# Scores of a windowed attention: the products with the keys' low halves on 64 rows of the array, two heads in different PSUM banks

## The chip, the cores and the metric

The kernel runs on one core of one Trainium2 chip. The metric is the device time of one execution in microseconds (us). Before the change the median of 3 runs is 1161.12 us (1160.22 to 1161.37). The engines are named as in the profile: PE is TensorE (the matrix array; PEld are its weight loads), DVE is VectorE, ACT is ScalarE, POOL is GpSimd, SP issues DMAs. L701 is line 701 of the kernel before.

## The reference

A decoder trunk of two layers over 512 tokens with 1024 features, all in fp32. Layer 0 mixes tokens by a gated position mix in chunks of 128, then a gated MLP with a short convolution, then a gated embedding. After it keys and values are made once. Layer 1 attends to them in a sliding window of 128 tokens, with 16 query heads in 4 groups that share 4 key heads of 64 features. The part that bears on the change is the attention:

```python
def mixer_b(xn, w_q, sinks, w_o, kblk, vblk):
    q = (xn @ w_q).reshape(B, nb, BLOCK, N_KV_HEADS, GQA_GROUP, HEAD_DIM)
    scores = jnp.einsum('bnikgd,bnjkd->bnkgij', q, kblk) * (HEAD_DIM ** -0.5)
    ...
    scores = scores - slopes[:, :, None, None] * dist
    scores = jnp.where(valid[None, :, None, None], scores, -jnp.inf)
    m = jnp.maximum(jnp.max(scores, axis=-1, keepdims=True), sink)
    e = jnp.exp(scores - m)
    probs = e / (jnp.sum(e, axis=-1, keepdims=True) + jnp.exp(sink - m))
    out = jnp.einsum('bnkgij,bnjkd->bnikgd', probs, vblk)
    return out.reshape(B, S, N_Q_HEADS * HEAD_DIM) @ w_o
```

## The kernel before

Every fp32 operand of a large product is split in two float32r tiles, a high half and the rest, the low half, and a product is the sum of three: high by high, low by high, high by low. `mm3` (L176 to L184) and `mm3t` (L186 to L195) do this for the dense layers; weights are streamed from HBM into raw tiles (L135), and split by ACT (L155) and DVE (L156) a few units ahead of their use.

The attention is done in 16 steps, 4 groups of heads by 4 blocks of 128 queries. `scores(i)` makes the scores of the 4 heads of one group for one block, `weights(i)` divides by the sums, `turn(i)` transposes the weights on TensorE (L733) and splits them, and `mix(i)` multiplies by the values (L756). They are staggered: in round i of the loop come `scores(i)`, then a piece of other work from `fill(i)` (projections of later queries, `values`, and in the last rounds parts of the output product), then `mix(i - 2)`, `turn(i - 1)` and `weights(i)`. Scores, turns and weights are given a high priority, so the program's scheduler may put them ahead of the filler; the order on an engine is fixed when the program is built, and each engine works in that order.

In `scores` a head's contraction is only 64 features long, so the 128 rows of the array hold two things for it. The tile `q` of head e (of 4 in its group) has the high half of its 64 features on one side of the partitions, `sides[e % 2]` (0 to 63 or 64 to 127), and their low half on the other side (L593 to L608). The keys' high half `kh` and low half `kl` are kept twice, on both sides (L579 to L584). So one product of 128 rows, `q` by `kh` (L698), gives high by high plus low by high, and a second, `q` by `kl` (L699), gives high by low plus low by low. A block of scores has 256 keys (the block before and the own one), or 128 for the first block. One PSUM bank holds the scores of two heads, 0 and 1 in the first, 2 and 3 in the second, 256 columns each. A bank is taken from a pool of 8 that all parts of the kernel share.

After a head's two products one DVE instruction (L701) adds the distance penalty, masks, and reduces to the head's smallest negated score, `neg`; in the program it stands between this head's products and those of the next. Then ACT takes the exponential of each head with its sum (L706), and `ds` gathers what the sink adds (L709, L710).

The order of heads that the scheduler made of this in most steps: products of heads 0 and 2 first, then, once the reduction of head 0 has read its bank, head 1, and then head 3.

Of the kernel before, what the change touches and what calls it, by code (L numbers as in the profile page):

```python
# [13 lines left out]
P = 128  # L14
# [12 lines left out]
GQ = HEADS // GROUPS  # L27
# [21 lines left out]
def tile_yoco(ctx: ExitStack, tc: tile.TileContext, t, out: bass.AP, out_b: bass.AP):  # L49
    nc = tc.nc  # L50
# [10 lines left out]
    def psum(name):  # L61
        return mmp.tile([P, S], F32, tag="mm", name=name)
# [250 lines left out]
    def slope(hd):  # L313
        return 2.0 ** (-8.0 * (hd + 1) / HEADS)
# [152 lines left out]
    far = const.tile([P, 2 * P], F32, name="far")  # L467
# [40 lines left out]
    for c in range(4):  # L508
# [4 lines left out]
        for j in range(2):  # L513
# [7 lines left out]
            for b in range(NC):  # L521
                nc.tensor.matmul(sp[:, b * P : (b + 1) * P], zv[b][:, m * P : (m + 1) * P], wsT[:, m, :],
                                 start=True, stop=True)
# [33 lines left out]
    kh = [mp.tile([P, 2, S], F32R, tag=f"m{j}", name=f"kh{j}") for j in range(2)]  # L557
    kl = [mp.tile([P, 2, S], F32R, tag=f"m{2 + j}", name=f"kl{j}") for j in range(2)]
    sides = [slice(0, HD), slice(HD, P)]
# [50 lines left out]
    qs = {0: []}  # L610
# [73 lines left out]
    def scores(i):  # L684


        g, n = steps[i]
        k0 = 0 if n else P
        nk = 2 * P - k0
        t0 = (n - 1) * P + k0  # L690
        pr = mp.tile([P, GQ, 2 * P], F32, tag=f"m{4 + i % 2}", name=f"pr{i}")
        neg = at.tile([P, GQ], F32, tag="neg", bufs=2, name=f"neg{i}")
        for e in range(GQ):
            if e % 2 == 0:
                sc = psum(f"sc{i}_{e}")
            o = sc[:, (e % 2) * 256 : (e % 2) * 256 + nk]
            q = qs[g][e][:, n * P : (n + 1) * P]
            nc.tensor.matmul(o, q, kh[g // 2][:, g % 2, t0 : t0 + nk], start=True, stop=False)  # L698
            nc.tensor.matmul(o, q, kl[g // 2][:, g % 2, t0 : t0 + nk], start=False, stop=True)  # L699
            hd = GQ * g + e  # L700
            nc.vector.tensor_tensor_reduce(out=pr[:, e, :nk], in0=far[:, k0:], in1=o, scale=-slope(hd),  # L701
                                           scalar=nsink[:, hd : hd + 1], op0=ALU.add, op1=ALU.min,
                                           accum_out=neg[:, e : e + 1])
        sm = at.tile([P, GQ], F32, tag="sm", bufs=2, name=f"sm{i}")
        for e in range(GQ):
            nc.scalar.activation(pr[:, e, :nk], pr[:, e, :nk], AF.Exp, bias=neg[:, e : e + 1], scale=-1.0,  # L706
                                 accum_out=sm[:, e : e + 1])
        ds = at.tile([P, GQ], F32, tag="ds", bufs=2, name=f"ds{i}")
        nc.vector.tensor_add(ds, sink[:, GQ * g : GQ * (g + 1)], neg)  # L709
        nc.scalar.activation(ds, ds, AF.Exp)  # L710
        live[i] = (pr, nk, sm, ds)
# [57 lines left out]
    for i in range(last + 2):  # L769
        if i < last:  # L770
            with tc.high_priority():
                scores(i)
        fill(i)
        if i >= 2:
            mix(i - 2)
        if 0 <= i - 1 < last:
            with tc.high_priority():
                turn(i - 1)
        if i < last:
            with tc.high_priority():  # L780
                weights(i)
# [199 lines left out]
```

## Time and profile before

| | |
|---|---|
| median of 3 runs | 1161.12 us |
| the profiled execution | 1160.82 us |
| its span, from the first to the last instruction | 1159.1 us |
| mean granted TensorE clock | 0.998 |
| high products, L698: 48 of 256 columns, 16 of 128 | 589.2 to 688.8 us |
| reductions, L701 | 591.2 to 689.4 us |

The times on the last two lines count from the start of the span, as all times of the trace do. A row of a timeline has the start, the duration, the engine, the line, the operation, output and inputs by the program's names, and the shape: 128*128 128x256 is a stationary operand of 128 by 128 and a moving one of 256 columns. Records of products overlap each other, since the array is pipelined and their ends are modelled; how far apart two starts lie is what a product costs. Where an engine was idle before an instruction, the brackets at the end of the row name the time and what released it.

### The profile page before, as it was taken

Reading aid. Unit: us, or ns where it says so; the run is one execution under the profiler, and the core shown is the slowest. Engines: PE = TensorE matmul, PEld = TensorE weight load, DVE = VectorE, ACT = ScalarE, POOL = GpSimd, SP = SyncE. Lnnn points to the kernel's source line nnn. Section 1 sums busy time; section 2 is a strip of 40 time slices with the busy share of each in tenths; the row PEclk is TensorE's granted clock in tenths of the full one; section 3 lists DMA queues with packets and bytes.
Section 4 is the critical chain, followed back from the end, with each engine's and each line's share of the span. In section 5 each row is a group of like instructions: output and inputs, shape, how many; then the busy total and the mean of one; then the engine's idle time right before and its main releaser. Section 6 shows DMA issues by size and latency. Waiting matters only on the chain.

```text
span 1159.1 us, 13846 instructions
## 1 busy us (share of the span) xinstructions
PE 1145.6 (99%) x5464; PEld 962.0 (83%) x5464; DVE 742.9 (64%) x1165; ACT 530.7 (46%) x860; POOL 78.4 (7%) x87
## 2 busy tenths in 40 slices
PE   9999999999999999999999999999999999999997
PEld 7888888888888888888888888888888888888896
DVE  7356477763676367556877876677636773675665
ACT  6534344431344244544667874544413432344542
POOL 2000300000000000031200002100000000000222
PEclk9999999999999999999999999999999999999999
DMA  9321322322322323232133214232232232224302
GB/s 321 122 75 73 109 77 106 109 76 107 109 67 97 109 92 120 82 109 107 37 92 110 77 53 174 80 109 85 97 109 84 90 100 109 91 89 148 109 1 73
DMA packets 30736, 115.42 MB, mean 100 GB/s; under 512 B 3016, under 2 KB 14928, under 8 KB 21200
## 3 DMA queue, kind: packets, MB, share of 16 engines
q1 hardware_dynamic: 29552, 113.37, 28.9%
q10 hardware_dynamic: 1120, 1.18, 0.3%
q8 instruction: 43, 0.70, 0.2%
q14 instruction: 21, 0.17, 0.0%
HBM read 108.24 MB, written 2.11 MB: 95 GB/s over the span
## 4 chain that ended last, share of the span: by engine, by line
PE 95%; DVE 2%; DMA 1%; ACT 1%; issue 1%; POOL 0%; SPq 0%; POOLq 0%; ACTq 0%
PE up L184 14%; PE up L182 14%; PE up L183 14%; PE d L183 8%; PE d L184 8%; PE d L182 8%; PE gate L182 2%; PE gate L183 2%; PE gate L184 2%; PE pv L756 1%; PE o L182 1%; PE v L193 1%; PE v L194 1%; PE o L183 1%; PE o L184 1%; PE u L182 1%
## 5 line engine op out<-in xcount | busy, mean ns | idle before, releaser
L156 DVE TENSOR_TENSOR wl<-wraw,wh 128x1024 fp32r<-128x1024 f32 (+2 forms) x197 | 239.3, 1217 | 135.0 <-ACT wh L155 134.5
L155 ACT CAST wh<-wraw 128x1024 fp32r<-128x1024 f32 (+1 forms) x196 | 202.3, 1034 | 265.9 <-PE d L183 131.5
L182 PE MATMUL up<-nf00h,wh 128*128 128x512 f32 x352 | 137.2, 390 | 0.0
L182 PE MATMUL up<-nf10h,wh 128*128 128x512 f32 x352 | 137.1, 389 | 0.0
L184 PE MATMUL up<-nf00h,wl 128*128 128x512 f32 x352 | 137.0, 389 | 0.0
L184 PE MATMUL up<-nf10h,wl 128*128 128x512 f32 x352 | 137.0, 389 | 0.0
L183 PE MATMUL up<-nf00l,wh 128*128 128x512 f32 x352 | 136.9, 389 | 0.0
L183 PE MATMUL up<-nf10l,wh 128*128 128x512 f32 x352 | 136.9, 389 | 0.0
L182 PE MATMUL d<-ah,wh 128*128 128x512 f32 x352 | 136.9, 389 | 0.0
L183 PE MATMUL d<-al,wh 128*128 128x512 f32 x352 | 136.9, 389 | 0.0
L184 PE MATMUL d<-ah,wl 128*128 128x512 f32 x352 | 136.9, 389 | 0.0
L351 ACT ACTIVATE c<-hs,vec 128x512 f32<-128x512 f32 x88 | 71.6, 816 | 71.7 <-DVE hs L347 71.1
L352 DVE SCALAR_TENSOR_TENSOR c<-hs,vec,c 128x511 f32<-128x511 f32 x88 | 65.8, 749 | 34.6 <-ACT c L351 34.5
L327 DVE TENSOR_TENSOR h<-h,d 128x512 f32<-128x512 f32 x56 | 38.5, 687 | 73.7 <-PE d L184 73.7
L240 ACT CAST ah<-a 128x512 fp32r<-128x512 f32 x44 | 27.4, 623 | 109.5 <-DVE a L357 109.4
L182 PEld LDWEIGHTS up<-nf10h,wh 128*128 128x128 f32 x352 | 66.1, 188 | 13.8
L183 PEld LDWEIGHTS up<-nf00l,wh 128*128 128x128 f32 x352 | 66.1, 188 | 13.8
L182 PEld LDWEIGHTS d<-ah,wh 128*128 128x128 f32 x352 | 66.1, 188 | 13.8
L183 PEld LDWEIGHTS up<-nf10l,wh 128*128 128x128 f32 x352 | 66.1, 188 | 13.7
L183 PEld LDWEIGHTS d<-al,wh 128*128 128x128 f32 x352 | 66.1, 188 | 13.7
L184 PEld LDWEIGHTS up<-nf00h,wl 128*128 128x128 f32 x352 | 66.1, 188 | 13.7
L184 PEld LDWEIGHTS d<-ah,wl 128*128 128x128 f32 x352 | 66.1, 188 | 13.7
(337 smaller groups left out, 2089.4 us busy)
## 6 DMA issues: line engine op xcount, KB each, us to landing
wraw<-in_w_up SPq DMA_DIRECT2D x44, 1024.0 KB, 4.8
wraw<-in_w_down SPq DMA_DIRECT2D x16, 896.0 KB, 4.6
wraw<-in_w_down SPq DMA_DIRECT2D x8, 1024.0 KB, 4.9
wraw<-in_w_u SPq DMA_DIRECT2D x4, 1024.0 KB, 5.7
wraw<-in_w_out SPq DMA_DIRECT2D x4, 1024.0 KB, 4.8
wraw<-in_w_gate SPq DMA_DIRECT2D x4, 1024.0 KB, 4.8
wraw<-in_w_q SPq DMA_DIRECT2D x4, 1024.0 KB, 5.6
wraw<-in_w_o SPq DMA_DIRECT2D x4, 1024.0 KB, 5.4
```

The source lines that it names most:

```text
L155: nc.scalar.copy(wh[:, :n], src)
L156: nc.vector.tensor_sub(wl[:, :n], src, wh[:, :n].bitcast(F32))
L182: nc.tensor.matmul(ps, wh[:, a:b], xh, start=st, stop=False)
L183: nc.tensor.matmul(ps, wh[:, a:b], xl, start=False, stop=False)
L184: nc.tensor.matmul(ps, wl[:, a:b], xh, start=False, stop=en)
L193: nc.tensor.matmul(ps, xh[:, s], wh[:, a:b], start=st, stop=False)
L194: nc.tensor.matmul(ps, xl[:, s], wh[:, a:b], start=False, stop=False)
L240: nc.scalar.copy(hi, src)
L327: nc.vector.tensor_add(h[m], h[m], ps)
L351: nc.scalar.activation(c, hs, AF.Identity, bias=v("conv_b", l * 2 * NJ + col), scale=cw[2])
L352: nc.vector.scalar_tensor_tensor(c[:, 1:], hs[:, : S - 1], cw[1], c[:, 1:], op0=ALU.mult, op1=ALU.add)
L756: nc.tensor.matmul(ps, lhs, rhs[:, :, e, :], start=first, stop=end)
```

## The change

In `scores` both banks are taken at the start, and the heads are dealt to them in turn: 0 and 2 in the first, 1 and 3 in the second. All eight products come first, in the order of the list: with `kh` for heads 0 and 1, with `kl` for heads 0 and 1, and the same for heads 2 and 3. Those with `kh` use all 128 rows as before. Those with `kl` use only the 64 partitions of `sides[e % 2]`, where the head's high half lies: head 0 on partitions 0 to 63 and head 1 on 64 to 127, one after the other into different banks. The product of the query's low half with the keys' low half is so left out. The four reductions follow after the eight products.

```diff
+        banks = [psum(f"sc{i}_{b}") for b in range(2)]
+        out_ = [banks[e % 2][:, e // 2 * 256 : e // 2 * 256 + nk] for e in range(GQ)]
+        cols = slice(n * P, (n + 1) * P)
+        for e in (0, 1, 4, 5, 2, 3, 6, 7):
+            me = slice(0, P) if e < GQ else sides[e % 2]
+            ks = (kh if e < GQ else kl)[g // 2]
+            nc.tensor.matmul(out_[e % GQ], qs[g][e % GQ][me, cols], ks[me, g % 2, t0 : t0 + nk],
+                             start=e < GQ, stop=e >= GQ)
         for e in range(GQ):
-            if e % 2 == 0:
-                sc = psum(f"sc{i}_{e}")
-            o = sc[:, (e % 2) * 256 : (e % 2) * 256 + nk]
-            q = qs[g][e][:, n * P : (n + 1) * P]
-            nc.tensor.matmul(o, q, kh[g // 2][:, g % 2, t0 : t0 + nk], start=True, stop=False)
-            nc.tensor.matmul(o, q, kl[g // 2][:, g % 2, t0 : t0 + nk], start=False, stop=True)
             hd = GQ * g + e
-            nc.vector.tensor_tensor_reduce(out=pr[:, e, :nk], in0=far[:, k0:], in1=o, scale=-slope(hd),
+            nc.vector.tensor_tensor_reduce(out=pr[:, e, :nk], in0=far[:, k0:], in1=out_[e], scale=-slope(hd),
                                            scalar=nsink[:, hd : hd + 1], op0=ALU.add, op1=ALU.min,
                                            accum_out=neg[:, e : e + 1])
```

## The prediction

> **What bounds the kernel now.** I read the page first: the table of engines, and the shares of the chain that ended last.
>
> ```profile
> PE 1145.6 (99%) x5464; PEld 962.0 (83%) x5464; DVE 742.9 (64%) x1165; ACT 530.7 (46%) x860; POOL 78.4 (7%) x87
> ...
> PE 95%; DVE 2%; DMA 1%; ACT 1%; issue 1%; POOL 0%; SPq 0%; POOLq 0%; ACTq 0%
> ```
>
> TensorE (PE) has work nearly always, and 95% of the chain is its own. So the change is worth what it takes from, or adds to, TensorE's time in the one stage that it touches; time of other engines counts only where TensorE waits for it. Next, the table of stretches, for the attention stage and for its busiest quarter. Columns: length, then busy time and count of PE, PEld (weight loads), DVE, ACT, POOL, then granted clock, DMA share and GB/s.
>
> ```profile
> 664.00:690.00 26.00, 24.86 (x161) 21.78 (x160) 22.06 (x83) 21.34 (x72) 0.00 (x0) 1.00 0.21 62
> ...
> 589.00:702.00 113.00, 109.66 (x701) 97.21 (x700) 88.80 (x296) 85.73 (x258) 0.00 (x0) 1.00 0.28 82
> ```
>
> Here TensorE lacks 113.00 - 109.66 = 3.34 us by its records, and those overlap each other, so the real slack is larger. DVE reaches 22.06/26.00 = 85% and ACT 21.34/26.00 = 82% from 664 to 690: these two are close behind TensorE, closer than their 64% and 46% over the whole span say. The clock is full, so it plays no part. The third view is the line of the products with the keys' high halves, with what TensorE waited for ahead of them.
>
> ```profile
> L698 PEld LDWEIGHTS sc<-kh,q x64: 186/188/193, 589.2 to 688.8; 128*128 128x128 f32 x64
> L698 PE MATMUL sc<-kh,q x64: 220/306/388, 589.3 to 689.0; 128*128 128x256 f32 x48, 128*128 128x128 f32 x16
> ...
>   DVE neg L701: 4.2, 11
>   issue: 2.1, 2
>   DVE q L598: 1.8, 2
>   DMA q<-qf: 1.6, 2
> ```
>
> There are 64 such products: 48 with 256 columns (12 steps of 4 heads) and 16 with 128 (the first step of each of the 4 groups). The largest wait, 4.2 us in 11 places, is for "DVE neg L701": the reduction of another head. It comes from the layout: two heads share a PSUM bank, and the second head's product is held until the reduction has read the first out of that bank.
>
> **The change, part by part.** *(1) The low products themselves.* 64 products stay 64. Their columns stay, only rows 64 to 127 or 0 to 63 are dropped, so each alone takes the time it took. A gain needs two of them to run at once. This is the pace of products with 256 columns, a waiting one among them:
>
> ```profile
> 613.04 0.28 PE L193 MATMUL vv<-wh,n10h 128*128 128x256 f32 x1
> 613.16 0.28 PE L194 MATMUL vv<-wh,n10l 128*128 128x256 f32 x1
> 613.28 0.28 PE L195 MATMUL vv<-wl,n10h 128*128 128x256 f32 x1
> 613.49 0.38 PE L698 MATMUL sc<-kh,q 128*128 128x256 f32 x1
> 613.72 0.28 PE L699 MATMUL sc<-kl,q 128*128 128x256 f32 x1
> 613.83 0.28 PE L193 MATMUL vv<-wh,n10h 128*128 128x256 f32 x1
> ```
>
> Unhindered they start 0.12 us apart (613.04, 613.16, 613.28). And this is the pace of weight loads where products with 128 columns leave them no cover:
>
> ```profile
> 590.46 0.19 PEld L698 LDWEIGHTS sc<-kh,q 128*128 128x128 f32 x1 [0.98 <-DVE q L598]
> 590.57 0.19 PEld L699 LDWEIGHTS sc<-kl,q 128*128 128x128 f32 x1
> 590.68 0.19 PEld L194 LDWEIGHTS vv<-wh,n10l 128*128 128x128 f32 x1
> 590.79 0.19 PEld L195 LDWEIGHTS vv<-wl,n10h 128*128 128x128 f32 x1
> ```
>
> One load follows another after 0.11 us, and every low product still needs its own load. If two half-height loads also go one after the other, a pair costs 2 x 0.11 = 0.22 us against 2 x 0.12 = 0.24: it saves 0.02 us, over the 24 pairs of 256 columns about 0.5 us, and nothing over the 8 pairs of 128 columns, which loads bound already. If two half-height loads and both products go at once, each pair saves a whole slot: 24 x 0.12 + 8 x 0.11 = 3.8 us. Those are the ends for this term. No row shows two loads at once, and the nearest rows show them in file, so I take 0.5 us. The Trainium skill ("TensorEngine Tiling (Array Packing)", Key Properties) says that different tiles of the array can run loads and matmuls in parallel; by it this term would be the 3.8 us, which is the second rival. No row here has a half-height product, so the trace can't say.
>
> Neighbours in the program needn't be neighbours on the engine. The order on TensorE at 611.56:
>
> ```profile
> 611.56 0.36 PE L698 MATMUL sc<-kh,q 128*128 128x256 f32 x1
> 611.76 0.28 PE L699 MATMUL sc<-kl,q 128*128 128x256 f32 x1
> 611.88 0.28 PE L698 MATMUL sc<-kh,q 128*128 128x256 f32 x1
> 612.00 0.27 PE L733 MATMUL tr<-ident,pr 128*128 128x128 f32 x1
> 612.03 0.36 PE L699 MATMUL sc<-kl,q 128*128 128x256 f32 x1
> 612.23 0.38 PE L733 MATMUL tr<-ident,pr 128*128 128x128 f32 x2
> ```
>
> A transpose of the step before has slipped between the high and the low product of one head. Where one slips between two low products, that pair has no partner; so even with parallel loads some of the 3.8 us goes.
>
> *(2) Going to half height and back.* With the new order a step goes from full rows to half rows and back twice: 4 x 16 = 64 switches. The nearest switch in this trace is to a part of the columns, the two transposes "turned" with 8 stationary columns (128*8):
>
> ```profile
> 146.25 0.39 PE L184 MATMUL d<-ush,wl 128*128 128x512 f32 x1
> 146.48 0.38 PE L543 MATMUL turned<-ident,vec 128*8 128x128 f32 x2
> 146.62 0.48 PE L182 MATMUL up<-nf00h,wh 128*128 128x512 f32 x1
> 146.93 0.40 PE L183 MATMUL up<-nf00l,wh 128*128 128x512 f32 x1
> ...
> 691.59 0.87 PE tr L733 x8
> ```
>
> The last row, from the chain, prices a transpose at 0.87/8 = 0.11 us, and the first two rows price a product with 512 columns at 0.23. From 146.25 to 146.93 are two such products and two such transposes: 2 x 0.23 + 2 x 0.11 = 0.68 us, and 0.68 us passed. Leaving and re-entering the full array cost nothing there, nor did "turned" wait for the record before it to end at 146.64. So I take 0. The upper bound: had a switch to let the array run empty, it would cost what a 256-column record is longer than its slot, 0.28 - 0.12 = 0.16 us, and with a load that can't start early 0.10 more (next part); 64 x 0.26 = 16.6 us. The Trainium skill (same page, Key Properties) states that changing the tiling mode drains the array; by that rule the sum would be higher by the 10 us worked out in the third rival. The rows at 146.48 don't bear it out for columns; for rows nothing here shows it.
>
> *(3) The waits inside a step.* All eight products of a step now come ahead of its four reductions, so no product waits for a reduction of its own step. That takes away the 4.2 us. It takes away something else: at 613.49 the product that waited runs 613.72 - 613.49 = 0.23 us to the next instead of 0.12. Its load couldn't start ahead of the wait, so 0.11 us of load is exposed. At most two products a step wait like that, 32 x 0.11 = 3.5 us. So the term lies between 0 (every wait comes back elsewhere) and 4.2 + 3.5 = 7.7 us; below nothing it could go only by the new waits of part (4). I take the middle, 3.8 us: what TensorE does right after these products are transposes and value products whose inputs DVE and ACT make, and those two, at 85% and 82% of the stage's end now, would stand near 90% if the stage shrank by 5 us, so some of the waits return under other names.
>
> *(4) What is added.* Head 0's reduction used to need two products; now, as banks are guarded whole (that is why the second head waits today), it needs all four of its bank, the last of which is the seventh issued: five more slots, 0.6 us later. Queued behind it on DVE are the step's other reductions, and ACT's exponentials wait for them. In return the reductions run without a stop: in the chain, one from 667.93 releases a subtraction, then a DMA, then TensorE:
>
> ```profile
> 667.93 0.48 DVE pr L701
> 668.42 0.60 DVE qf L603
> 669.05 2.83 DMA q<-qf
> 672.02 0.30 PE sc L698
> ...
> L701 DVE CUSTOM_DVE_ANT_0 pr<-far,sc,nsink x64: 337/475/483, 591.2 to 689.4; 128x256 f32<-128x256 f32 x48, 128x128 f32<-128x128 f32 x16
> ```
>
> Four reductions at 0.48 us are 1.9 us in file; today the second pair starts only after another round of products. I set 0.6 us later at the start against an earlier end, at 0 for TensorE; what covers it is the filler of projections and merges between the steps. Without that cover it would be 16 x 0.6 = 9.6 us lost, but the filler stays as it is. The first step of a group also has its queries by DMA (1.6 us of waits above): heads 2 and 3 there need later queries than heads 0 and 1, before as after, so that stays. Both banks are taken at once rather than one by one: the second is wanted one product sooner, 0.12 us, against banks that were held over two rounds; 0. No DMA, no instruction of DVE, ACT, POOL or SP is added or removed, so no queue is passed.
>
> *The sum.* The profiled execution took 1160.82 us, of which 1159.1 is its span. 1160.82 - 0.5 - 3.8 = 1156.5 us. The median of the runs is 0.3 us above that execution, so 1156.8; I forecast 1157.0 us, 4.1 us or 0.36% below the median.
>
> **The rivals.** *The waits come back* (0.2): the 4.2 us reappear ahead of transposes and value products, for DVE and ACT. For it speaks their 85% and 82%; against it, the idle time ahead of transposes in the groups of the stage (the last number), which is nothing today:
>
> ```profile
> L733 PE MATMUL tr<-ident,pr 128*128 128x128 f32 x102 | 17.0, 273 | 0.0
> ```
>
> Time: 1161.1 - 0.5 = 1160.6, and anything down to 2.3 us below the median.
>
> *The pairs do run side by side* (0.18): then 3.8 us in place of 0.5, and with the waits 1161.1 - 3.8 - 3.8 = 1153.5 us. Against it speak the loads in file at 590.46 and the transpose inside a pair at 612.00.
>
> *Half height costs* (0.2), the slower side: each switch between full and half rows lets the array run empty or exposes a load. It decides from the point where a switch costs more than (3.8 + 0.5)/64 = 0.07 us. With an exposed load alone, 64 x 0.11 = 7.0 us: 1161.1 + 7.0 - 3.8 = 1164.3. With the drained tail of 0.16 instead, 10.2 us: 1167.5 (the skill's rule of the drain gives this one). Against it: "turned" paid nothing. For it: that was columns, and a load for half the rows may have to leave the other half alone until its product has started.
>
> *The change doesn't do what it says*, that is, no two low products ever overlap, is inside my forecast: that counts on 0.5 us of it only.
>
> **How the numbers follow.** The forecast has 0.42, the waits that come back 0.2, side by side 0.18, half height costs 0.2. The forecast's own range, by the ends of part (3) less what returns, is 1154.5 to 1159.0. The range for 8 in 10 runs from 1153.0, which takes in the side-by-side case, to 1165.0, which takes in the cheaper half of the slower rival; left out are its drained half and some of the far end below, together under 0.2. About 0.2% (2.3 us) is what a measurement of this kernel can tell from no change. Faster by more than that: the forecast's 0.42 less 0.03 at its upper end, plus 0.18, so 0.57. Within it: most of the waits that come back plus that 0.03, 0.22. Slower: 0.21.
>
> **What would show it.** In the changed profile the high products' list of waits has no "DVE neg" of the own step, and the time before them falls from 4.2 us to under 1; if transposes or value products show new waits on DVE or ACT of some 3 us, the first rival holds. Two low products of one pair that start within 0.02 us, with the next product 0.12 us after, mean side by side; starts 0.11 apart mean loads in file. A high product that starts 0.2 us or more after a low one with no wait named means that half height costs. The last value product of the stage starts here:
>
> ```profile
> 701.50 0.28 PE L756 MATMUL pv<-pts,vtl 128*128 128x256 f32 x1
> ```
>
> From the first score product at 589.3 that is 112.2 us; the forecast is wrong if this stretch isn't shorter by 2 us at least.

## The result, and the profile after

The changed kernel takes 1170.02 us (median of 5 runs, 1169.16 to 1171.11), the kernel before 1161.37 us in the same runs: 1.0075 times as long, 95% interval 1.0064 to 1.0086, so 8.7 us slower. The forecast was 1157.0 us. The profiled execution took 1171.11 us, its span 1169.4 us. Its table of engines:

```profile
PE 1157.5 (99%) x5464; PEld 965.3 (83%) x5464; DVE 742.5 (63%) x1165; ACT 529.1 (45%) x860; POOL 78.2 (7%) x87
```

The counts are those of before and the other engines' times are within 2 us of them on DVE and ACT; TensorE (PE) is busy 12 us longer with the same 5464 products. The line of the score products, now L701, shows what replaced the waits:

```profile
L701 PEld LDWEIGHTS sc<-kh,q x64: 186/190/329, 589.4 to 696.9; 128*128 128x128 f32 x64
L701 PE MATMUL sc<-kh,q x64: 220/314/387, 589.6 to 696.9; 128*128 128x256 f32 x48, 128*128 128x128 f32 x16
L701 PEld LDWEIGHTS sc<-kl,q x64: 182/183/183, 589.8 to 697.2; 64*128 64x128 f32 x64
L701 PE MATMUL sc<-kl,q x64: 322/380/385, 589.8 to 697.2; 64*128 64x256 f32 x48, 64*128 64x128 f32 x16
...
  DVE q L598: 2.2, 4
  issue: 1.2, 4
  DMA q<-qf: 0.2, 1
```

"DVE neg" is gone from the list: the 4.2 us of waits for reductions went, as meant (what that number adds up is told further down). But the low products (64*128) have a median record of 380 ns, where those on all rows had 282, though half of the array's rows have nothing to do. The order of products in the third step, on TensorE and on its weight loads, shows why:

```profile
614.59 0.48 PE L701 MATMUL sc<-kh,q 128*128 128x256 f32 x2
615.00 0.38 PE L701 MATMUL sc<-kl,q 64*128 64x256 f32 x2
615.31 0.50 PE L701 MATMUL sc<-kh,q 128*128 128x256 f32 x2
615.74 0.38 PE L701 MATMUL sc<-kl,q 64*128 64x256 f32 x1
616.05 0.33 PE L737 MATMUL tr<-ident,pr 128*128 128x128 f32 x1
616.31 0.38 PE L701 MATMUL sc<-kl,q 64*128 64x256 f32 x1
616.62 0.44 PE L737 MATMUL tr<-ident,pr 128*128 128x128 f32 x2
616.82 0.36 PE L760 MATMUL pv<-pts,vth 128*128 128x256 f32 x1
```

```profile
615.00 0.19 PEld L701 LDWEIGHTS sc<-kl,q 64*128 64x128 f32 x2
615.31 0.30 PEld L701 LDWEIGHTS sc<-kh,q 128*128 128x128 f32 x2
615.74 0.18 PEld L701 LDWEIGHTS sc<-kl,q 64*128 64x128 f32 x1
```

Two things can be read here. The two low products at 615.00 fill one record's time, 0.38 us for both, and their two loads take 0.19 us for both, the time of one: they do run side by side. And the loads behind a change of rows begin with their product (615.00 and 615.00, 615.31 and 615.31) instead of ahead of it; from the pair at 615.00 to the next product are 0.31 us, where a slot, the time from one start to the next, is 0.12. This is the sign that the prediction named for its third rival: a high product that starts 0.2 us or more after a low one, with no wait named. In the second half of the step a transpose at 616.05 has come between the two low products, so this pair is two products alone, and the step has six changes of rows where the order in the kernel's text has four. The stage, from the first score product to the last value product, runs here from 589.56 to this row:

```profile
711.89 0.28 PE L760 MATMUL pv<-pts,vtl 128*128 128x256 f32 x1
```

That is 122.3 us against 112.2 before, 10.1 us longer; the two profiled spans differ by 1169.4 - 1159.1 = 10.3 us, so the loss lies in this stage.

### The profile page after: what moved, and what is told of

It reads as the page before. It is cut to its first block, busy times and chain, and to the rows that moved or that the text cites. A ratio compares the mean times of both kernels' runs of the same rounds, so it can differ in the third digit from the quotient of the medians.

```text
span 1169.4 us, 13856 instructions
## 1 busy us (share of the span) xinstructions
PE 1157.5 (99%) x5464; PEld 965.3 (83%) x5464; DVE 742.5 (63%) x1165; ACT 529.1 (45%) x860; POOL 78.2 (7%) x87
## 4 chain that ended last, share of the span: by engine, by line
PE 94%; DVE 2%; issue 1%; DMA 1%; ACT 1%; POOL 0%; SPq 0%; POOLq 0%; DVEq 0%; ACTq 0%
PE up L182 14%; PE up L184 14%; PE up L183 14%; PE d L182 8%; PE d L183 8%; PE d L184 8%; PE sc L701 2%; PE pv L760 2%; PE gate L182 2%; PE gate L184 2%; PE gate L183 2%; PE u L182 1%; PE u L183 1%; PE u L184 1%; PE o L183 1%
## 5 line engine op out<-in xcount | busy, mean ns | idle before, releaser
L184 PEld LDWEIGHTS up<-nf10h,wl 128*128 128x128 f32 x352 | 66.1, 188 | 13.9
L182 PEld LDWEIGHTS up<-nf00h,wh 128*128 128x128 f32 x352 | 66.1, 188 | 13.7
```

The lines of the kernel that those rows point to most:

```text
L182: nc.tensor.matmul(ps, wh[:, a:b], xh, start=st, stop=False)
L184: nc.tensor.matmul(ps, wl[:, a:b], xh, start=False, stop=en)
```

## The experiments

The theory after the result: *each change between full and half rows empties the array and exposes the next load*. Counted in the order that TensorE was given, which the expectations call the program's order, the changed kernel has 92 such changes (28 low products alone, 18 pairs: 46 runs of half rows, in and out). The rival: the new order of heads and the later reductions cost the time.

**e1: the same order, all rows.**

```diff
-            me = slice(0, P) if e < GQ else sides[e % 2]
+            me = slice(0, P)
```

> The changed kernel with one word undone: the low products take all 128 rows again (low by low is then in the scores, as before the change). The order of instructions on every engine is that of the changed kernel. Theory (each switch between full and half rows costs about 0.19 us, 92 switches in the program's order, less 18 pairs side by side at 0.12 us): 92 x 0.19 - 18 x 0.12 = 15.3 us are gone, 1170.0 - 15.3 = 1154.7 us, faster than before by some 6 us. Rival (the new order and the later reductions cost the time): 1170 us, no change from the changed kernel. Rival (both): between 1161 and 1170.

Measured: 0.9963 of before, interval 0.995 to 0.9976, some 4.3 us faster than before and 13.0 us faster than the changed kernel; 6 and 15.3 us were expected. The instructions of every engine stand in the same order as in the changed kernel, so half rows alone cost the 13.0 us, and the rival falls. The same eight products and three transposes as above:

```profile
611.41 0.48 PE L701 MATMUL sc<-kh,q 128*128 128x256 f32 x2
611.74 0.40 PE L701 MATMUL sc<-kl,q 128*128 128x256 f32 x2
611.97 0.40 PE L701 MATMUL sc<-kh,q 128*128 128x256 f32 x2
612.21 0.28 PE L701 MATMUL sc<-kl,q 128*128 128x256 f32 x1
612.33 0.28 PE L737 MATMUL tr<-ident,pr 128*128 128x128 f32 x1
612.36 0.36 PE L701 MATMUL sc<-kl,q 128*128 128x256 f32 x1
612.56 0.38 PE L737 MATMUL tr<-ident,pr 128*128 128x128 f32 x2
612.70 0.36 PE L760 MATMUL pv<-pts,vth 128*128 128x256 f32 x1
```

From the first high product to the value product that follows are 612.70 - 611.41 = 1.29 us here, and 616.82 - 614.59 = 2.23 us with half rows: 0.94 us for six changes of rows and one pair side by side.

**e2 and e3: more and fewer changes of rows.** The changed kernel with another order; in e3 the accumulation flags follow it.

```diff
-        for e in (0, 1, 4, 5, 2, 3, 6, 7):
+        for e in (0, 4, 1, 5, 2, 6, 3, 7):
```

> The changed kernel with the order kh, kl of head 0, then of head 1, 2, 3: every low product stands alone, 128 switches and no pair side by side. Theory: 128 x 0.19 = 24.3 us over e1, 1179 us, 9 us slower than the changed kernel. Rival (order and reductions): reductions wait for the same eight products, so about 1170. Rival (a half-height product is itself slow, whatever stands beside it): 64 of them as in the changed kernel, 1170.

```diff
-        for e in (0, 1, 4, 5, 2, 3, 6, 7):
+        for e in range(2 * GQ):
...
-                             start=e < GQ, stop=e >= GQ)
+                             start=e < 2, stop=e >= 6, skip_group_check=True)
```

> The changed kernel with the four high products first, then the four low ones: 52 switches in the program's order. Theory: 52 x 0.19 = 9.9 us less some 15 pairs at 0.12, so 8 us over e1: 1163 us. Rival (a half-height product is itself slow): 1170. Rival (order and reductions): 1170 or a little above.

Measured: e2 1.0146 (1.0132 to 1.0159), e3 1.0009 (1.0000 to 1.0018). Against e1, at 1161.8 us of before:

| | changes of rows | slots saved by pairs | over e1, us | us for a change |
|---|---|---|---|---|
| e1 | 0 | 0 | 0 | |
| e3 | 52 | 26 | 5.3 | (5.3 + 3.1) / 52 = 0.16 |
| changed kernel | 92 | 18 | 13.0 | (13.0 + 2.1) / 92 = 0.16 |
| e2 | 128 | 0 | 21.3 | 21.3 / 128 = 0.17 |

The slots saved are counted in the same order and priced at 0.118 us. The intervals of the ratios leave about 2 us in each difference, which is 0.02 to 0.04 us in the last column. The loss follows the number of changes, not the 64 half-height products, which are the same in all three. The expectations of 1179 and 1163 us came out (1179.03 and 1162.85 us), but as totals only: they started from an e1 of 1154.7 us and a price of 0.19 us, and both were off.

**e4 and e9: the price by itself.** Rows of products on ones at the start of the kernel before, whose output nothing reads. Two of the rows of e9:

```diff
...
+    for _ in range(8):
+        nc.tensor.matmul(*one(ps, full), start=True, stop=True)
+        nc.tensor.matmul(*one(ps, lo), start=True, stop=True)
...
+    for _ in range(6):
+        nc.tensor.matmul(*one(ps, full), start=True, stop=True)
+        for _ in range(4):
+            nc.tensor.matmul(*one(ps, lo), start=True, stop=True)
+            nc.tensor.matmul(*one(ps2, hi), start=True, stop=True)
...
```

> The kernel before with nine short rows of products on ones put in at its start, read from the trace alone: full products; full and half rows in turn; pairs of half rows in two banks; half rows on one side only; full, half, half; full and 64 columns in turn; full and 8 columns in turn; full and half rows with 512 columns; full with 512 columns and 8 stationary columns in fp32. Theory (only a change of rows empties the array): 0.12 us per product in the first row; some 0.5 us for a full and a half product in the second, of which 0.38 are two switches; 0.12 per pair in the third; 0.12 in the fourth; the two rows with fewer columns cost nothing extra. Rival (any change of the array's shape empties it): the rows with 64 and 8 columns cost as much as the second. Rival (a switch is dearer behind a longer product): more than 0.38 us in the row with 512 columns.

> The kernel before with rows of products put in at its start, each on lines of its own, with 16 full products of 512 columns between them so that the clock stays full; read from the trace alone. Full and half rows in turn (L248, L249): 0.31 us from each to the next. Full, half, half in two banks (L252 to L254): 0.63 us a round, the two halves 0.005 apart. Full and four pairs (L257 to L260): if a pair costs one slot, 0.12 + 4 x 0.12 + 2 x 0.2 = 1.0 us a round against 9 x 0.12 = 1.07 with full rows, so four pairs in a run just pay. Half and quarter rows (L263, L264): theory (any change in the number of rows empties the array) 0.31; rival (only full against part) 0.12. Full float32r and full fp32 (L267, L268), full and fp32 transposes (L271, L272): if a change of type empties the array, 0.2 us more than the slots. Full and transposes of 8 columns (L275, L276), the form of the two transposes on which the prediction's zero rested: 0.12 + 0.11, no extra. Full and transposes on 64 rows (L279, L280): 0.2 us per change, as for any product on half rows.

From the timeline of e9, full and half rows in turn, then one round of a full product and four pairs:

```profile
9.96 0.38 PE L249 MATMUL idle<-idle 64*128 64x256 f32 x1
10.28 0.38 PE L248 MATMUL idle<-idle 128*128 128x256 f32 x1
10.59 0.38 PE L249 MATMUL idle<-idle 64*128 64x256 f32 x1
...
31.01 0.38 PE L257 MATMUL idle<-idle 128*128 128x256 f32 x1
31.33 0.38 PE L259 MATMUL idle<-idle 64*128 64x256 f32 x1
31.33 0.38 PE L260 MATMUL idle<-idle 64*128 64x256 f32 x1
31.55 0.28 PE L259 MATMUL idle<-idle 64*128 64x256 f32 x1
31.55 0.28 PE L260 MATMUL idle<-idle 64*128 64x256 f32 x1
31.67 0.28 PE L259 MATMUL idle<-idle 64*128 64x256 f32 x1
31.67 0.28 PE L260 MATMUL idle<-idle 64*128 64x256 f32 x1
...
32.00 0.39 PE L257 MATMUL idle<-idle 128*128 128x256 f32 x1
```

In turn, each product takes 0.31 us instead of 0.12, so a change costs 0.19 to 0.20. The halves of a pair start together. The second pair starts 0.22 us after the first, and from there on a pair takes one slot of 0.12. A round of one full product and four pairs takes 32.00 - 31.01 = 0.99 us, against 9 x 0.118 = 1.06 on full rows: at four pairs in a run half rows begin to pay, by 0.07 us. With a single pair between full products a round takes 0.63 us, as expected (L252 to L254).

The transposes with 8 columns, on which the prediction rested, in turn with full products, and transposes on 64 rows:

```profile
63.47 0.27 PE L276 MATMUL idle<-ident,idle 128*8 128x128 f32 x1
63.49 0.36 PE L275 MATMUL idle<-idle 128*128 128x256 f32 x1
63.70 0.27 PE L276 MATMUL idle<-ident,idle 128*8 128x128 f32 x1
...
69.58 0.27 PE L280 MATMUL idle<-ident,idle 64*128 64x64 f32 x1
...
70.09 0.27 PE L280 MATMUL idle<-ident,idle 64*128 64x64 f32 x1
```

A round with 8 columns takes 63.70 - 63.47 = 0.23 us, two plain slots; a round with 64 rows takes 70.09 - 69.58 = 0.51. A change of type alone costs nothing either: in turn with full float32r products, transposes in fp32 take 0.23 us a round, and fp32 products, which have two records each, 0.34 (0.12 + 2 x 0.11). Half against quarter rows, where no full product is near:

```profile
40.46 0.38 PE L263 MATMUL idle<-idle 64*128 64x256 f32 x1
40.77 0.38 PE L264 MATMUL idle<-idle 32*128 32x256 f32 x1
```

0.31 us again: it isn't only the full array that costs to leave; both changes in the number of rows that were tried cost the same. From e4, the stretches with 16 products each (the counts include a neighbour): full and half rows of 256 columns in turn; full and 64 stationary columns in turn, both with 256 moving columns; full and half rows of 512 columns in turn. The last stretch holds five slots of products on 64 rows of one side alone. Columns: length, busy time and count of PE, granted clock, DMA share, GB/s.

```profile
8.51:13.40 4.89, 4.89 (x17) 1.00 1.07 372
24.58:26.45 1.87, 1.87 (x17) 1.00 0.12 33
29.30:36.00 6.70, 6.70 (x18) 1.00 0.00 0
17.68:18.28 0.60, 0.60 (x7) 1.00 1.09 346
```

1.87/16 = 0.117 us: fewer columns cost nothing here, and full float32r products in turn with such of 8 columns took 0.118. 6.70/16 = 0.42 us, 0.19 more than a slot of 0.23: the price doesn't grow with the length of the product. 0.60/5 = 0.12 us: half rows that aren't left take a plain slot, so a half-height product isn't slow in itself.

The last row of e4 doesn't fit the theory that only rows count: full products of 512 columns in turn with fp32 products of 8 stationary columns. These are the weight loads of the 8 columns:

```profile
36.88 0.10 PEld L232 LDWEIGHTS idle<-idle 128*8 128x8 f32 x2 [0.35 <-issue]
...
37.62 0.10 PEld L232 LDWEIGHTS idle<-idle 128*8 128x8 f32 x2 [0.24 <-issue]
```

A round takes 37.62 - 36.88 = 0.74 us, where the plain slots come to 0.23 + 2 x 0.11 = 0.45. Neither the type alone nor 8 columns alone cost anything in the rows above; why both together cost 0.29 us a round stays open. The kernel has no such products, and its "turned" are transposes.

**e5 and e6: where the 4.3 us of e1 come from.** All rows, all products ahead of the reductions; e5 with the banks of before, e6 with a bank for each head.

```diff
-        out_ = [banks[e % 2][:, e // 2 * 256 : e // 2 * 256 + nk] for e in range(GQ)]
+        out_ = [banks[e // 2][:, e % 2 * 256 : e % 2 * 256 + nk] for e in range(GQ)]
...
-        for e in (0, 1, 4, 5, 2, 3, 6, 7):
-            me = slice(0, P) if e < GQ else sides[e % 2]
+        for e in (0, 4, 1, 5, 2, 6, 3, 7):
+            me = slice(0, P)
```

> e1 with the banks and the order of heads of before (heads 0 and 1 in the first bank, kh and kl of a head one after the other, all rows), but all eight products still ahead of the reductions. Theory (e1 gains because no product waits for a reduction of its own step): the same gain as e1, 0.996 to 0.997 of before. Rival (the dealing of heads to banks gains it): 1.000. Rival (reductions come late in e1): head 0's reduction is ready two products sooner here, so faster than e1, 0.994.

> e5 with a bank of its own for each head, four of the eight banks in a step, all rows: a reduction needs only its own two products. Theory (TensorE has the filler while the reductions start late, so late reductions cost nothing): as e1, 0.996 to 0.997, or slower where four banks are missing elsewhere. Rival (late reductions cost 0.6 us a step, 16 x 0.6 = 9.6 us at most): some us faster than e1, 0.990 to 0.994.

Measured: e5 0.9965 (0.9951 to 0.9978), e6 0.9975 (0.9966 to 0.9985). The dealing of heads to banks gains nothing: e5 has that of before and gains as much as e1. An earlier start of the reductions shows no gain in e6, but e6 doesn't settle it: with four banks in a step its weight loads wait for banks that are still in use, 1.1 us in 2 places for a reduction and 1.0 us in one for a value product. What the three kernels share is that all products of a step are issued ahead of its reductions, so that none waits for a reduction of its own step.

**e7 and e8: all pairs kept together.** `turn(i - 1)` without its high priority, in e3 (e7) and in the same with all rows (e8); both have one order on all engines.

> e3 with the transposes of the step before at normal priority, so that fewer of them slip between the low products: 38 switches, 13 runs of four low products and 6 of two, that is 32 pairs side by side. Against e8, whose order on every engine is the same. Theory (0.16 us a switch, 0.12 us a pair): 38 x 0.16 - 32 x 0.12 = 2.2 us slower than e8. Rival (with every pair side by side half rows pay): 3.8 us faster than e8.

> e7 with the low products on all 128 rows (low by low is then in the scores). Theory: about as e1, 0.996 to 0.998 of before, since the transposes wait a little longer for their turn; 2.2 us faster than e7. Rival: slower than e7 by 3.8 us.

Measured: e7 1.0006 (0.9997 to 1.0015), e8 0.998 (0.9971 to 0.999): half rows cost 0.0026 x 1161.8 = 3.0 us (some 1.5 either way) even with every pair side by side and 38 changes of rows; the sum forecast 2.2. Half rows don't pay in any order that was tried, and e1 beats both kernels.

## Why the prediction was wrong

**The step that failed is (2), "So I take 0".** It took the two "turned" transposes as the nearest switch. They change the columns, and e9 shows that the form itself is free: 0.23 us a round however often it is repeated. A change of rows costs 0.19 to 0.20 us by itself and 0.16 to 0.17 on average in the kernel; why it is less there, perhaps because some changes fall on loads that a wait had exposed anyway, isn't shown. That lies within the bounds that the step set, 0 to 0.26 us. The row was read rightly; what it was carried over to was another thing. The Trainium skill ("TensorEngine Tiling (Array Packing)", Key Properties: a change of the tiling mode drains the array) fits the price for rows, 0.31 us against 0.12 in e9; for columns no price showed with float32r products in e4, 0.117 us a product, nor with the transposes of e9, and one of 0.29 us a round with the fp32 products of e4. What the rows show is a late load and the price; that the array itself runs empty is argued.

The same step counted 64 changes, "4 x 16", from the order in the program's text. Part (1) had itself shown a transpose between a high and its low product at 612.00, but only the lost partner was counted, not that a low product left alone has an entry and an exit of its own. 92 x 0.16 = 15 us is the term that was set at 0. It is also why the third rival, which named the mechanism, fell short: with 64 changes it gave 1164.3 and 1167.5 us. Its two prices of a switch, 0.11 and 0.16 us, were near: 92 x 0.16 would have given it 1161.1 + 14.7 - 3.8 = 1172.0 us.

**(1) was too cautious.** It took loads to go in file, because full-height loads do, and 0.5 us in all. Half-height loads of different rows go at once and the products start together (615.00; 31.33 in e9), as the Trainium skill says of tiles in the same section. It is worth one slot a pair, 18 x 0.118 = 2.1 us: the 3.8 us less the 14 pairs that were parted.

**(3) was right in its direction, and its size was partly luck.** The waits for reductions went, and the term of 3.8 us measured 4.3 us in e1 (2.8 to 5.8 by the interval). But the "4.2, 11" that it started from adds the idle time of two engines, weight loads and products:

```profile
PEld sc L698 <- DVE neg L701: 3.4, 10, 1.0
...
PE sc L698 <- DVE neg L701: 0.8, 1, 0.8
```

The products themselves sat idle for a reduction once, 0.8 us; the ten waits of 3.4 us are late loads, and the 3.5 us of exposed loads that the prediction put on top probably count some of the same waits a second time. So 7.7 us was no bound that the rows gave, and that its middle lies near the 4.3 us is in part chance. How that gain divides between waits and late loads isn't shown. The first rival, waits that come back for DVE and ACT, didn't come: ahead of transposes and value products e1 has one wait of 0.2 us, of a load. At score products it waits for queries, counted the same way 2.3 us for DVE and 1.3 us for DMA.

**(4)** set the later reductions and the banks at nothing. Nothing contradicts it: e1 and e5 gain with late reductions. What an earlier start would be worth with banks to spare wasn't measured.

So the sum by what was measured is -4.3 + 15.1 - 2.1 = 8.7 us, where the prediction had -3.8 + 0 - 0.5. It closes by its making, since the 15.1 us are the 13.0 us of e1 and the 2.1 us of the pairs; with the bare price of e9, 92 x 0.19 = 17.5, it would be 11.1 us.

## What to carry to other kernels

Two products on half the rows do run as one, but going there and back costs about 0.4 us, as much as three to four products of 256 columns: by the rows of e9, pack only where four pairs or more follow each other unbroken (no kernel here has such a run), and count the changes in the order that the engine gets, after the scheduler, not in the program's text. Where an accumulator bank holds two results, issue all its products ahead of the first read: that alone took about 4 us off this kernel (e5). A row of the trace prices what it shows: a switch of columns says nothing of a switch of rows.

## What was not expected of the hardware

In the profiled execution of the changed kernel the granted clock fell to half for about 3.4 us in the first steps of the attention. Two of the microseconds: length, busy time and count of PE, granted clock, DMA share and GB/s.

```profile
593.00:594.00 1.00, 1.00 (x8) 0.59 0.88 115
594.00:595.00 1.00, 1.00 (x6) 0.50 0.35 147
```

Half a clock for 3.4 us is 1.7 us lost, part of the 122.3 us of the stage; e1 shows a clock of 1.00 from 590 to 597. The profile of e2 has the same drop from 592 to 596, that of e7 one from 673 to 676, and those of before, e3, e5, e6 and e8 have none in the stage. In e4 it fell once and in e9 three times in or behind rows of products with changes of rows. But in e9 it fell a fourth time, in the attention, where no product has fewer rows:

```profile
742.22 0.30 PE L747 MATMUL sc<-kh,q 128*128 128x128 f32 x1 [1.39 <-DMA q<-qf]
...
743.00:746.00 3.00, 3.00 (x10) 0.51 0.00 0
```

There TensorE had just sat idle for 1.39 us, in e7 for 1.36 us shortly before its drop, and in the changed kernel for 0.58 and 0.39 us. So a change of rows isn't needed for a drop, and whether it can bring one about isn't shown. The mean clock of single runs goes from 0.996 to 0.999 for the kernel before as well. None of this is in the bare price of 0.19 us, which was read at a clock of 1.00.
